# The first stage of a decoder step: DVE and ScalarE in a written order, and the dt scaling ahead of a convolution

## The chip, the cores and the metric

The kernel runs on one core of a Trainium2 chip. Time is device microseconds of one execution, and less is better. The engines are TensorE (PE in the profile, with PEld for its weight loads), VectorE (DVE), ScalarE (ACT), GpSimd (POOL) and SyncE (SP, which issues most DMAs).

## The reference

One layer of a hybrid decoder for a prompt of 1024 tokens and a sample group of 8 x 8 tokens, 1088 tokens in all, with a model width of 1024. All inputs are float32.

```python
def rmsnorm(x, g):
    y = xf * lax.rsqrt(jnp.mean(xf * xf, axis=-1, keepdims=True) + EPS)
    return y * g

h = rmsnorm(x, g1)
proj = h @ w_in                       # 1024 -> 2824 columns
u, v, bgate, cgate, hb, z, xbc, dt_raw = split(proj)
ya = chunk_mlp(gelu(u), gelu(v))      # mixer A
yb = bgate * conv3(cgate * hb)        # mixer B
xbc = silu(conv4(xbc))                # mixer C: x, B, C
dt = softplus(dt_raw + dt_bias)
y = ssd(xs, dt, -exp(a_log), Bm, Cm, state) + d_skip * xs
yc = rmsnorm(y * silu(z), ssm_norm)
x = x + concat([ya, yb, yc]) @ w_out
x = x + square(relu(rmsnorm(x, g2) @ w_ff1)) @ w_ff2
out = rmsnorm(x, final_norm)          # and the new states
```

The change is in the first stage: `rmsnorm(x, g1)`, the first columns of `h @ w_in`, and `dt_raw`.

## The kernel before

**Layout.** Activations lie transposed, features on the 128 partitions and the 1088 tokens along the free dimension. x comes as eight tiles `xt` of 128 x 1088, one for each block of 128 features (k = 0 to 7). Tokens are worked on in three chunks `CH` of 364, 364 and 360.

**Precision.** A product of float32 numbers is made of three faster ones. Each operand is split into a high part (rounded to the format of the fast product) and a low part, the rest; PE adds up high x high, low weight x high x, and high weight x low x. For x the high part is `g1 * x` rounded, written to half 0 of the tile `big`, and the low part is `g1 * x` minus it, in half 1 (L262, DVE). The high part is made by DVE for k = 0 to 2 and by ACT for k = 3 to 7 (L259 and L257). For weights `split_w` copies the high part on ACT (L100) and subtracts on DVE (L101). The first weight block, w0, is split in two pieces of 256 and 768 columns, the later ones (w1, w2, ...) in one.

**RMSNorm.** The scaling by 1/rms of a token is put off: the projection runs on `g1 * x`, and its result is multiplied by `rstd` afterwards. For `rstd`, ACT squares each x tile (L232; in place, except for k = 0, whose square starts the sum `ss`), and DVE adds the other seven squares to `ss` (L236). PE then sums `ss` over the partitions with a matrix of ones (`rms_scale`, L172), ACT takes the logarithm and the exponential (L173, L177), and DVE does one Newton step for each chunk (L180 to L183).

**The first projections.** `dt_products(k)` computes `dt_raw` from xt[k] in float32 (L247, 12 records in the profile for each k) into one bank, `psd`. The first projection (weights w0, feature block 4 of mixer C's convolution input) goes over k with all three chunks' banks open (L336 for the high weights, L340 for the low ones), so that it can follow x as it comes. `rstd` isn't known yet, so ACT copies the three banks out unscaled into a buffer `cb` (L345), and `dt_raw` into `dtT` (L347, L348). The second projection (w1, block 5) goes chunk by chunk through the helper `mm3` (L131, L132, L133); its first chunk has a bank of the pool `aps`, the others one of the three of the pool `gps`. After that chunk `rms_scale` is issued. When `rstd` is there, DVE empties the second projection's banks with the scaling in it (L293), multiplies the first projection's copies by it (L354, four products), runs the convolution of block 4 on ACT and DVE (L307, then three steps L310), multiplies `dtT` by `rstd` (L358 and L360, eight small products), and then convolves block 5. During the third projection (block 6) PE turns `dtT` to tokens on partitions (`dt_tokens`, L382 and L387), from which `softplus` makes dt.

**What sets the order.** Each engine works off its own queue in order. The order of the queues comes from a planner when the program is built: at each step an engine takes, among the instructions that the planner holds to be ready, the one that stands first in the program's text. Waits between engines are then put in. Inside `with tc.manual_schedule(engines=...)` the named engines keep the order of the text instead; before, the kernel has this only in its last stage. The x tiles, the constants `cp` and the first weights are loaded by DMAs that are all issued in the first few microseconds, and w1 and w2 behind them.

The names of the lines: L94 load of a weight block, L100 and L101 its split, L131 to L133 projection by chunks, L172 to L183 `rstd`, L232 square, L236 sum of squares, L247 dt products, L257, L259 and L262 high and low parts of x, L336 and L340 first projection, L345 its copy, L293 scaled emptying of a bank, L307 and L310 convolution, L354 scaling of the copy, L358 and L360 scaling of `dtT`, L382 dt to tokens.

Of the kernel before, what the change touches and what calls it, by code (L numbers as in the profile page):

```python
# [7 lines left out]
F32 = mybir.dt.float32  # L8
F32R = mybir.dt.float32r
BF16 = mybir.dt.bfloat16  # L10
AF = mybir.ActivationFunctionType
ALU = mybir.AluOpType
# [3 lines left out]
P = 128  # L16
D = 1024
KT = D // P
# [4 lines left out]
T = SEQ + TS  # L23
# [39 lines left out]
HC = (0, 256, 1024)  # L63
# [8 lines left out]
def body(nc, tc, I, O):  # L72
    ctx = ExitStack()
    V, S, G, PE, SY = nc.vector, nc.scalar, nc.gpsimd, nc.tensor, nc.sync
# [3 lines left out]
    whlp = ctx.enter_context(tc.tile_pool(name="whlp", bufs=2))  # L78
# [7 lines left out]
    big = bigp.tile([P, KT * 2 * T], F32R, name="big")  # L86

    def C(name):
        o, n = PCOLS[name]
        return cp[:, o:o + n]  # L90
# [3 lines left out]
        SY.dma_start(out=st, in_=src)  # L94
        return st

    def split_w(st, cuts=(0, 1024), pool=None):
        w = (pool or whlp).tile([P, 2, 1024], F32R, name="whl")
        for a, b in zip(cuts, cuts[1:]):
            S.copy(out=w[:, 0, a:b], in_=st[:, a:b])  # L100
            V.tensor_tensor(out=w[:, 1, a:b], in0=st[:, a:b], in1=w[:, 0, a:b].bitcast(F32),  # L101
                            op=ALU.subtract)
        return w

    w_plan = [I["w_in"][f] for f in W_IN_ORDER] + [I["w_out"][f] for f in range(KT)] * 2
    w_st, w_sp = {}, {}
# [5 lines left out]

    def w_split(i):
        if i < len(w_plan) and i not in w_sp:
            w_sp[i] = split_w(w_st[i], HC if i == 0 else (0, 1024))

    def next_w():

# [83 lines left out]
    rstd = statp.tile([P, T], F32, name="rstd")  # L202
# [8 lines left out]
    xg = []  # L211
    xts = []
    for k in range(KT):
        xt = midp.tile([P, 1112], F32, name="xt", tag="mid")
        xts.append(xt)
        if k == 0:
            SY.dma_start(out=xt[:, :364], in_=I["xT"][k][:, :364])
            S.dma_start(out=cp[:, :PC_A], in_=I["cpack"][:, :PC_A])
            st0 = w_st[0] = wstp.tile([P, 1024], F32, name="wst")
# [10 lines left out]
    def square(k):  # L230
        xt = xts[k][:, :T]
        S.activation(out=ss if k == 0 else xt, in_=xt, func=AF.Square)  # L232

    def add_square(k):
        if k > 0:
            V.tensor_tensor(out=ss, in0=ss, in1=xts[k][:, :T], op=ALU.add)  # L236

    V.tensor_tensor(out=wdt[:, :, 0:8], in0=C("wdt").rearrange("p (k m) -> p k m", m=8),
                    in1=C("g1").unsqueeze(2).broadcast_to([P, KT, 8]), op=ALU.mult)
# [3 lines left out]
    def dt_products(k):  # L243

        parts = [(j, 0, DTQ, j * DTQ) for j in range(4)] + [(j, DTQ, 32, SEQ + 32 * j) for j in range(2)]
        for j, o, n, t in parts:
            PE.matmul(psd[32 * j:32 * j + 32, o:o + n], wdt[:, k], xts[k][:, t:t + n],  # L247
                      start=k == 0 and o == 0, stop=k == KT - 1, skip_group_check=True)

    for k in range(KT):  # L250
        xt = xts[k]
        dt_products(k)
        b = big[:, k * 2 * T:(k + 1) * 2 * T].rearrange("p (h t) -> p h t", h=2)
        g = C("g1")[:, k:k + 1]
        for a, e in (((0, 364), (364, T)) if k == 0 else ((0, T),)):
            if k > 2:
                S.activation(out=b[:, 0, a:e], in_=xt[:, a:e], func=AF.Identity, scale=g)  # L257
            else:
                V.tensor_scalar(out=b[:, 0, a:e], in0=xt[:, a:e], scalar1=g, scalar2=None, op0=ALU.mult)  # L259
        if k == 0:  # L260
            w_split(0)
        V.scalar_tensor_tensor(out=b[:, 1], in0=xt[:, :T], scalar=g, in1=b[:, 0].bitcast(F32),  # L262
                               op0=ALU.mult, op1=ALU.subtract)
        if k:
            square(k - 1)
        if k > 2:
            add_square(k - 2)
        xg.append(b)
    w_split(1)
    square(KT - 1)  # L270
    add_square(KT - 2)
    add_square(KT - 1)

    def evac_mul(c, ps, dst, rhs=None):
        rhs = rstd if rhs is None else rhs
# [3 lines left out]
    def pad_parts(buf, pad, src, c):  # L279

        c0, n = CH[c]
        if c < 2:
            return [(buf[:, pad + c0:pad + c0 + n], src[:, :n], lambda a: a[:, c0:c0 + n])]
        m, w = SEQ - c0, NJ + pad
        sb = buf[:, pad + SEQ:pad + SEQ + NB * w].rearrange("p (b w) -> p b w", w=w)
        rows = lambda a: a.rearrange("p (b w) -> p b w", w=NJ)
        return [(buf[:, pad + c0:pad + SEQ], src[:, :m], lambda a: a[:, c0:SEQ]),
                (sb[:, :, pad:], rows(src[:, m:n]), lambda a: rows(a[:, SEQ:T]))]
# [11 lines left out]
    def conv_c(i, buf):  # L300

        sb = buf[:, 3 + SEQ:].rearrange("p (b w) -> p b w", w=11)
        G.tensor_copy(out=stC[:, i, 0:3], in_=buf[:, SEQ:SEQ + 3])
        G.tensor_copy(out=stC[:, i, 3:27].rearrange("p (b w) -> p b w", w=3), in_=sb[:, :, 8:11])
        o = midp.tile([P, 1112], F32, name="xc", tag="mid")
        w = C("sconvw")[:, i * 4:i * 4 + 4]
        S.activation(out=o, in_=buf[:, 0:1112], func=AF.Identity, scale=w[:, 0:1],  # L307
                     bias=C("sconvb")[:, i:i + 1])
        for k in range(1, 4):
            V.scalar_tensor_tensor(out=o, in0=buf[:, k:k + 1112], scalar=w[:, k:k + 1], in1=o,  # L310
                                   op0=ALU.mult, op1=ALU.add)
        S.activation(out=o, in_=o, func=AF.Silu)
        G.tensor_copy(out=xcS[:, i].rearrange("p (b w) -> p b w", w=NJ),
                      in_=o[:, 1024:1112].rearrange("p (b w) -> p b w", w=11)[:, :, 3:11])
        mids[i] = o

    def new_buf(pad, prev):
        w = NJ + pad
        buf = cbp.tile([P, 1115], F32, name="cb", tag="cb")
        G.memset(buf[:, 0:pad], 0.0)  # L320
        G.tensor_copy(out=buf[:, pad + SEQ:pad + SEQ + NB * w].rearrange("p (b w) -> p b w", w=w)[:, :, 0:pad],
                      in_=prev.rearrange("p (b w) -> p b w", w=pad))
        return buf
# [7 lines left out]
    ps0 = [gp.tile([P, 512], F32, name="gps", tag="g") for _ in CH]  # L331
# [10 lines left out]
    buf = new_buf(3, C("sst")[:, 4 * 24:5 * 24])  # L342
    for c in range(3):
        for o, i, tok in pad_parts(buf, 3, ps0[c], c):
# [4 lines left out]
    buf5 = new_buf(3, C("sst")[:, 5 * 24:6 * 24])  # L349
    gemm(next_w(), xg, range(KT), lambda c, ps: evac_pad(c, ps, buf5, 3),  # L350
         first=ap.tile([P, 512], F32, name="aps", tag="a"), hooks=[lambda: rms_scale(aslots(), catp, "yb", ss, rstd, D, False)])
    for c in range(3):
        for o, i, tok in pad_parts(buf, 3, ps0[c], c):
            V.tensor_tensor(out=o, in0=o, in1=tok(rstd), op=ALU.mult)  # L354
    conv_c(4, buf)
    for j in range(4):
        r = slice(32 * j, 32 * j + 32)
        V.tensor_tensor(out=dtT[r, :DTQ], in0=dtT[r, :DTQ], in1=rstd[r, j * DTQ:(j + 1) * DTQ], op=ALU.mult)  # L358
        if j < 2:
            V.tensor_tensor(out=dtT[r, DTQ:], in0=dtT[r, DTQ:], in1=rstd[r, SEQ + 32 * j:SEQ + 32 * j + 32],  # L360
                            op=ALU.mult)
    conv_c(5, buf5)


# [359 lines left out]
    def norm_c():  # L724
        rms_scale(aslots(), tmpp, "t", ss, rstc, 512)
        for i in range(4):
# [9 lines left out]
                    in1=C("tri").unsqueeze(1).broadcast_to([P, 4, L]), op=ALU.mult)  # L736
    wms = am.tile([TS, 4, TS], F32, name="wms")
    V.tensor_tensor(out=wms, in0=cw[:TS, 4 * L:].rearrange("p (h t) -> p h t", t=TS),
                    in1=C("btri")[:TS].unsqueeze(1).broadcast_to([TS, 4, TS]), op=ALU.mult)
# [231 lines left out]
    raw, whl = {}, {}  # L971
# [650 lines left out]
```

## Time and profile before

| | |
|---|---|
| median of 3 runs | 1129.83 us (1129.47 to 1129.85) |
| the profiled execution | 1129.33 us, of which the span is 1127.5 |
| granted clock of TensorE | 0.999 |
| PE busy | 1116.2 us, 99% of the span |
| DVE busy | 836.0 us, 74% |
| ACT busy | 497.8 us, 44% |
| first projection on PE (from 7.73 us, with dt products) | ends at about 25 us |
| second projection's first chunk | to 30.4 us |
| `rstd` complete | 40.4 us |

A row of the time-ordered view has the start and the length of a group in us, the engine, the line of the kernel, the operation, the tile written and the tiles read, shapes, the count, and, in brackets, the idle time before it with what ended it. Matmuls are pipelined and their ends are modelled, so their spacing from start to start says more than their length. In a row of the view by stretches, a busy time is followed by the number of records. In the view of one tile or line, the DMA figures are the shortest, median and longest time from issue to landing.

### The profile page before, as it was taken

The numbers are of one execution on the slowest core, as the hardware profiler recorded it, in microseconds if no ns is written. First come the engines' busy times: TensorE is split into PE (matmuls) and PEld (weight loads), VectorE is DVE, ScalarE is ACT, GpSimd is POOL, SyncE is SP. The second block draws the span as 40 slices with busy tenths as digits, with TensorE's granted clock in tenths as the row PEclk, the third lists the DMA queues.
The fourth block names the chain that finished last, engine by engine and source line by source line (L and its number), as shares of the span: only waits on it lengthen the run. The fifth ranks groups of instructions, "written<-read, shape, count | busy, mean of one in ns | idle before, by whom it ended". The sixth has DMA issues, their size and how long they took to land.

```text
span 1127.5 us, 19980 instructions
## 1 busy us (share of the span) xinstructions
PE 1116.2 (99%) x8540; PEld 1097.5 (97%) x8540; DVE 836.0 (74%) x1111; ACT 497.8 (44%) x659; POOL 57.2 (5%) x94
## 2 busy tenths in 40 slices
PE   8999999999999999999999999999999999999997
PEld 6999999999999999999999999999999999999997
DVE  8875587865656476989697497497497496599786
ACT  7536273423563344753342542442443443443544
POOL 1110020110000000000000000000000000000015
PEclk9999999999999999999999999999999999999999
DMA  6112232321037353692853953953953953953504
GB/s 258 53 57 62 64 112 102 114 79 53 23 106 266 92 216 124 287 390 79 309 200 111 401 193 122 392 192 135 389 185 137 384 188 140 391 179 138 225 1 159
DMA packets 34776, 200.43 MB, mean 178 GB/s; under 512 B 4736, under 2 KB 7680, under 8 KB 27776
## 3 DMA queue, kind: packets, MB, share of 16 engines
q1 hardware_dynamic: 32592, 196.30, 47.2%
q10 hardware_dynamic: 2096, 2.85, 0.7%
q8 instruction: 67, 1.10, 0.4%
q14 instruction: 21, 0.17, 0.0%
HBM read 175.58 MB, written 22.77 MB: 176 GB/s over the span
## 4 chain that ended last, share of the span: by engine, by line
PE 94%; DVE 3%; issue 1%; ACT 1%; DMA 1%; POOL 0%; SPq 0%; POOLq 0%; ACTq 0%; DVEq 0%
PE ps L1049 19%; PE ps L1050 19%; PE ps L1051 19%; PE gps L131 10%; PE gps L132 10%; PE gps L133 10%; PE aps L577 1%; PE aps L581 1%; DVE big L262 1%; DMA xt<-xT 1%; DVE xq L914 0%; PE p L1049 0%; PE aps L512 0%; PE ps L875 0%; PE p L1051 0%
## 5 line engine op out<-in xcount | busy, mean ns | idle before, releaser
L1049 PE MATMUL ps<-big,whl 128*128 128x272 f32 x1312 | 377.7, 288 | 0.2 <-DVE f L1131 0.2
L1050 PE MATMUL ps<-big,whl 128*128 128x272 f32 x1312 | 377.6, 288 | 0.0
L1051 PE MATMUL ps<-big,whl 128*128 128x272 f32 x1312 | 376.9, 287 | 0.0
L1049 PEld LDWEIGHTS ps<-big,whl 128*128 128x128 f32 x1312 | 247.2, 188 | 0.6 <-DVE f L1131 0.5
L1050 PEld LDWEIGHTS ps<-big,whl 128*128 128x128 f32 x1312 | 247.1, 188 | 0.0
L1051 PEld LDWEIGHTS ps<-big,whl 128*128 128x128 f32 x1312 | 246.8, 188 | 0.0
L131 PE MATMUL gps<-big,whl 128*128 128x360 f32 (+2 forms) x752 | 239.8, 319 | 0.5 <-ACT cb L345 0.5
L132 PE MATMUL gps<-big,whl 128*128 128x360 f32 (+2 forms) x752 | 236.8, 315 | 0.3 <-DVE whl L101 0.3
L133 PE MATMUL gps<-big,whl 128*128 128x360 f32 (+2 forms) x752 | 236.0, 314 | 0.0
L100 ACT CAST whl<-wq 128x1024 fp32r<-128x1024 f32 x92 | 96.5, 1050 | 221.6 <-PE ps L1051 133.8
L101 DVE TENSOR_TENSOR whl<-wq,whl 128x1024 fp32r<-128x1024 f32 x92 | 112.4, 1222 | 52.6 <-ACT whl L100 52.5
L131 PEld LDWEIGHTS gps<-big,whl 128*128 128x128 f32 x752 | 141.4, 188 | 1.8 <-ACT cb L345 1.0
L132 PEld LDWEIGHTS gps<-big,whl 128*128 128x128 f32 x752 | 141.4, 188 | 0.9 <-DVE whl L101 0.5
L133 PEld LDWEIGHTS gps<-big,whl 128*128 128x128 f32 x752 | 141.3, 188 | 0.1
L949 DVE TENSOR_TENSOR x<-x,ps 128x544 f32<-128x544 f32 x188 | 131.0, 716 | 7.7 <-PE ps L1051 6.7
L1051 PE MATMUL ps<-fo,whl 128*128 128x272 f32 x416 | 119.5, 287 | 0.0
L1049 PE MATMUL ps<-fo,whl 128*128 128x272 f32 x416 | 119.3, 287 | 0.0
L1050 PE MATMUL ps<-fo,whl 128*128 128x272 f32 x416 | 119.2, 287 | 0.0
L100 ACT CAST whl<-wst 128x1024 fp32r<-128x1024 f32 (+2 forms) x39 | 40.1, 1027 | 130.7 <-PE gps L133 81.9
L1049 PEld LDWEIGHTS ps<-fo,whl 128*128 128x128 f32 x416 | 78.3, 188 | 0.2 <-issue 0.2
L1051 PEld LDWEIGHTS ps<-fo,whl 128*128 128x128 f32 x416 | 78.2, 188 | 0.0
L1050 PEld LDWEIGHTS ps<-fo,whl 128*128 128x128 f32 x416 | 78.2, 188 | 0.0
(327 smaller groups left out, 1395.3 us busy)
## 6 DMA issues: line engine op xcount, KB each, us to landing
big<-xcd SPq DMA_DIRECT2D x47, 2176.0 KB, 9.7
wq<-w SPq DMA_DIRECT2D x66, 512.0 KB, 4.4
xcd<-big SPq DMA_DIRECT2D x7, 2176.0 KB, 7.5
wst<-w_in SPq DMA_DIRECT2D x21, 512.0 KB, 3.6
wst<-w_out SPq DMA_DIRECT2D x16, 512.0 KB, 3.6
x<-xT SPq DMA_DIRECT2D x8, 544.0 KB, 5.6
dec<-scr SPq DMA_DIRECT2D x8, 512.0 KB, 4.1
xt<-xT SPq DMA_DIRECT2D x7, 544.0 KB, 8.6
```

Source lines behind the costliest of these rows:

```text
L100: S.copy(out=w[:, 0, a:b], in_=st[:, a:b])
L101: V.tensor_tensor(out=w[:, 1, a:b], in0=st[:, a:b], in1=w[:, 0, a:b].bitcast(F32), op=ALU.subtract)
L131: PE.matmul(ps[:, :n], hi, xh, start=start, stop=False)
L132: PE.matmul(ps[:, :n], lo, xh, start=False, stop=False)
L133: PE.matmul(ps[:, :n], hi, xl, start=False, stop=stop)
L262: V.scalar_tensor_tensor(out=b[:, 1], in0=xt[:, :T], scalar=g, in1=b[:, 0].bitcast(F32), op0=ALU.mult, op1=ALU.subtract)
L577: PE.matmul(yps[hh * HD:(hh + 1) * HD, i * L:(i + 1) * L], w[:, h * HD:(h + 1) * HD], m[:, h], start=i == 0 and n == 0, stop=n == len(term ...
L581: PE.matmul(sps[:, g * 256:(g + 1) * 256], bt[:, g * P:(g + 1) * P], xw[:, g * 256:(g + 1) * 256], start=True, stop=True)
L949: V.tensor_tensor(out=out, in0=a, in1=b, op=o)
L1049: PE.matmul(o, hi, xh, start=start and k == 0, stop=False, skip_group_check=True)
L1050: PE.matmul(o, lo, xh, start=False, stop=False, skip_group_check=True)
L1051: PE.matmul(o, hi, xl, start=False, stop=k == ks - 1, skip_group_check=True)
```

## The change

The loop over k that made dt products, high part, low part, square and sum together is taken apart. `high`, `low`, `square` and `add_square` become steps of their own, and DVE and ACT are held to the order of the text in this block: dt products first in the text (they run on PE, whose order the planner still makes); high and low part of k = 0; w0's first 256 columns; the square of k = 0; high and low part of k = 1; w0's other columns; high part of k = 2, the square of k = 1, low part of k = 2; high and low parts of k = 3 to 7; the split of w1; the squares of k = 2 to 7; all sums. Which engine does which step is as before, and each step has the same size. Further down, the products of `dtT` with `rstd` come ahead of those of the first projection's copy and of the convolution of block 4, rather than behind them.

```diff
-    def split_w(st, cuts=(0, 1024), pool=None):
-        w = (pool or whlp).tile([P, 2, 1024], F32R, name="whl")
+    def split_w(st, cuts=(0, 1024), pool=None, w=None):
+        if w is None:
+            w = (pool or whlp).tile([P, 2, 1024], F32R, name="whl")
...
-            w_sp[i] = split_w(w_st[i], HC if i == 0 else (0, 1024))
+            w_sp[i] = split_w(w_st[i])
...
     for k in range(KT):
-        xt = xts[k]
-        dt_products(k)
-        b = big[:, k * 2 * T:(k + 1) * 2 * T].rearrange("p (h t) -> p h t", h=2)
+        xg.append(big[:, k * 2 * T:(k + 1) * 2 * T].rearrange("p (h t) -> p h t", h=2))
+
+    def high(k):
         g = C("g1")[:, k:k + 1]
         for a, e in (((0, 364), (364, T)) if k == 0 else ((0, T),)):
+            o, i = xg[k][:, 0, a:e], xts[k][:, a:e]
             if k > 2:
-                S.activation(out=b[:, 0, a:e], in_=xt[:, a:e], func=AF.Identity, scale=g)
+                S.activation(out=o, in_=i, func=AF.Identity, scale=g)
             else:
-                V.tensor_scalar(out=b[:, 0, a:e], in0=xt[:, a:e], scalar1=g, scalar2=None, op0=ALU.mult)
-        if k == 0:
-            w_split(0)
-        V.scalar_tensor_tensor(out=b[:, 1], in0=xt[:, :T], scalar=g, in1=b[:, 0].bitcast(F32),
-                               op0=ALU.mult, op1=ALU.subtract)
-        if k:
-            square(k - 1)
-        if k > 2:
-            add_square(k - 2)
-        xg.append(b)
-    w_split(1)
-    square(KT - 1)
-    add_square(KT - 2)
-    add_square(KT - 1)
+                V.tensor_scalar(out=o, in0=i, scalar1=g, scalar2=None, op0=ALU.mult)
+
+    def low(k):
+        V.scalar_tensor_tensor(out=xg[k][:, 1], in0=xts[k][:, :T], scalar=C("g1")[:, k:k + 1],
+                               in1=xg[k][:, 0].bitcast(F32), op0=ALU.mult, op1=ALU.subtract)
+
+    ET = mybir.EngineType
+    with tc.manual_schedule(engines={ET.DVE, ET.Activation}):
+        for k in range(KT):
+            dt_products(k)
+        high(0)
+        low(0)
+        w_sp[0] = whlp.tile([P, 2, 1024], F32R, name="whl")
+        split_w(st0, HC[:2], w=w_sp[0])
+        square(0)
+        high(1)
+        low(1)
+        split_w(st0, HC[1:], w=w_sp[0])
+        high(2)
+        square(1)
+        low(2)
+        for k in range(3, KT):
+            high(k)
+            low(k)
+        w_split(1)
+        for k in range(2, KT):
+            square(k)
+        for k in range(KT):
+            add_square(k)
...
-    for c in range(3):
-        for o, i, tok in pad_parts(buf, 3, ps0[c], c):
-            V.tensor_tensor(out=o, in0=o, in1=tok(rstd), op=ALU.mult)
-    conv_c(4, buf)
     for j in range(4):
         r = slice(32 * j, 32 * j + 32)
         V.tensor_tensor(out=dtT[r, :DTQ], in0=dtT[r, :DTQ], in1=rstd[r, j * DTQ:(j + 1) * DTQ], op=ALU.mult)
...
+    for c in range(3):
+        for o, i, tok in pad_parts(buf, 3, ps0[c], c):
+            V.tensor_tensor(out=o, in0=o, in1=tok(rstd), op=ALU.mult)
+    conv_c(4, buf)
     conv_c(5, buf5)
```

## The prediction

> **What bounds the kernel now.** I read the page's engine shares, then the chain that ended last, then TensorE's (PE's) waits over the whole span, then the first 55 us queue by queue. The first row gives, for each engine, busy time, share of the span and instructions; the second is the chain's share by engine; the rest is who PE waited for (us in total, times, longest).
>
> ```profile
> PE 1116.2 (99%) x8540; PEld 1097.5 (97%) x8540; DVE 836.0 (74%) x1111; ACT 497.8 (44%) x659; POOL 57.2 (5%) x94
> ```
> ```profile
> PE 94%; DVE 3%; issue 1%; ACT 1%; DMA 1%; POOL 0%; SPq 0%; POOLq 0%; ACTq 0%; DVEq 0%
> ```
> ```profile
> PE gps L131 <- ACT cb L345: 0.5, 1, 0.5
> PE gps L132 <- DVE whl L101: 0.3, 1, 0.3
> PE aps L382 <- DVE dtT L358: 0.3, 1, 0.3
> PE ps L875 <- POOL ss L1463: 0.3, 1, 0.3
> ```
>
> PE is the bound. A change on DVE and ScalarE (ACT) is worth what it takes from PE's waits. Later stages hold few of them (L875 is the longest of those), so what PE has gained by 60 us should reach the end. The waits that this change can touch are L131, L132 and L382. Here is PE around the first two (start, duration, line, count):
>
> ```profile
> 18.98 0.66 PE L336 MATMUL gps<-big,whl 128*128 128x364 f32 x3
> 19.57 0.69 PE L247 MATMUL aps<-xt,wdt 128*32 128x256 f32 x12
> 20.18 0.77 PE L336 MATMUL gps<-big,whl 128*128 128x364 f32 x3
> ...
> 22.78 1.16 PE L336 MATMUL gps<-big,whl 128*128 128x364 f32 x6
> 23.78 0.66 PE L340 MATMUL gps<-big,whl 128*128 128x364 f32 x3
> 24.28 0.66 PE L336 MATMUL gps<-big,whl 128*128 128x364 f32 x3
> 24.78 0.33 PE L131 MATMUL aps<-big,whl 128*128 128x364 f32 x1
> 25.64 0.80 PE L131 MATMUL gps<-big,whl 128*128 128x364 f32 x2 [0.53 <-ACT cb L345]
> 26.43 0.44 PE L132 MATMUL aps<-big,whl 128*128 128x364 f32 x1
> ```
>
> From start to start, twelve matmuls take 24.78 - 22.78 = 2.00 us, so one streams in 0.167 us, whatever its modelled duration. I count by that pitch.
>
> **Part 1: low parts sooner (high, low and squares in a written order).** Was PE short of work in the first projection? The stretch, its length, then busy time and records of PE, PEld, DVE, ACT and POOL, granted clock, DMA share and GB/s:
>
> ```profile
> 7.73:24.95 17.22, 17.22 (x154) 14.12 (x154) 17.08 (x15) 14.95 (x15) 2.27 (x2) 1.00 0.76 303
> ```
>
> No: busy 17.22 of 17.22 us, at the full granted clock. Of the 154 records 84 are dt products (seven groups of 12, each 20.18 - 19.57 = 0.61 us: 4.3) and 70 are projection matmuls (70 x 0.167 = 11.7), 16.0 in all. The missing 1.2 us go to the fifteen or so changes between dt products and projection: the three matmuls at 18.98 took 0.59 us where 0.50 is streaming. These changes follow the arrival of the input tiles, which the edit leaves alone. So low parts that come sooner feed a full engine: 0 us. If the planner put the dt products into one group, it could gain up to 1.2; if it scattered them more, it could lose as much. I take 0.
>
> **Part 2: second weights before most squares and sums.** The first projection's last matmul has streamed at 24.95 (24.78 + 0.167). Then the low part of the second weights, w1, is awaited until 26.43: 1.48 us, in which two matmuls of the next chunks (0.33) found a place. Lost: 1.15. In the written order w1 waits only for its tile and for the last high part. ACT's rows, then the landing of the x tiles, then that of the weights:
>
> ```profile
> 18.38 2.29 ACT L257 ACTIVATE big<-xt,cp 128x1088 fp32r<-128x1088 f32 x2
> 20.57 2.20 ACT L232 ACTIVATE xt<-xt 128x1088 f32<-128x1088 f32 x2
> 22.68 1.03 ACT L100 CAST whl<-wst 128x1024 fp32r<-128x1024 f32 x1
> ```
> ```profile
> 25.15 1.23 ACT L345 COPY cb<-gps 128x364 f32<-128x364 f32 x4
> ```
> ```profile
> L223 SPq DMA_DIRECT2D xt<-xT x7: 432/494/981, 1.7 to 6.0; - x7
> DMA to landing us min/median/max: 3.9/8.3/10.8
> ```
> ```profile
> 7.71 0.33 SPq L94 DMA_DIRECT2D wst<-w_in  x1
> ```
> ```profile
> DMA to landing us min/median/max: 3.5/3.9/10.3
> ```
>
> The last x tile is issued at 6.0 and none needs over 10.8 us, so it is there by 16.8; w1 is issued at 7.71 and, with 10.3 the longest of its kind, there by 18.0. ACT: last high part 16.8 to 18.0 (two in 2.29, one in 1.2), w1's high part to 19.05. DVE's rows of before:
>
> ```profile
> 22.70 1.34 DVE L262 SCALAR_TENSOR_TENSOR big<-xt,cp,big 128x1088 fp32r<-128x1088 f32 x1
> 23.96 1.28 DVE L236 TENSOR_TENSOR ss<-ss,xt 128x1088 f32<-128x1088 f32 x1
> 25.16 1.21 DVE L101 TENSOR_TENSOR whl<-wst,whl 128x1024 fp32r<-128x1024 f32 x1
> 26.30 2.67 DVE L236 TENSOR_TENSOR ss<-ss,xt 128x1088 f32<-128x1088 f32 x2
> ```
>
> So the last low part runs from 18.0 to 19.35 and w1's low part ends about 20.5, where before it ended at 26.37. PE's wait until 26.43 is gone: **-1.15 us**.
>
> **What is late next: the sums.** Before, ss ends at 28.97 and PE comes to it here:
>
> ```profile
> 30.36 1.99 PE L172 MATMUL aps<-ss,cp 128*128 128x364 f32 x6
> ```
>
> That margin of 1.39 us hid the sums. Now all seven stand behind w1's low part, each reading what the last one wrote. Followed by an independent instruction, a sum takes 1.20 (23.96 to 25.16). Two in a row take 2.67, so the second starts 1.39 after the first. Seven from 20.5 end at 20.5 + 6 x 1.39 + 1.28 = 30.1; at 1.20 each they would end at 28.95. I take 30.1, since the pair at 26.30 is the same instruction in the same dependence.
>
> [...]
>
> The squares don't hold the sums: six of them behind w1's high part, at 1.10 each, end at 19.05 + 6.6 = 25.65. ACT's copies out of the first banks (L345) start there rather than at 25.15 and are done by 26.9. PE wants those banks only after its first chunk of the second projection, which has a bank of its own and, with 24 matmuls, ends at 24.95 + 4.0 = 28.95. Later copies: 0 us, with 2 us of cover.
>
> So PE comes to L172 at 28.95, and ss is 1.15 us away. If the planner lets L172 stand right behind the chunk, PE waits all of that and part 2 is spent; if it puts matmuls of the next chunk ahead, PE waits for nothing. The trace of before can't tell; I take half: **+0.55**. Either way L172 starts at 30.1 rather than 30.36, and the chain to rstd moves by only 0.26 us.
>
> **Part 3: dt times rstd sooner.** PE, then DVE:
>
> ```profile
> 43.60 0.33 PE L133 MATMUL gps<-big,whl 128*128 128x364 f32 x1
> 44.22 0.84 PE L382 MATMUL aps<-cp,dtT 128*128 128x8 f32 x6 [0.29 <-DVE dtT L358]
> ```
> ```profile
> 39.88 0.53 DVE L183 SCALAR_TENSOR_TENSOR rstd<-rt,rstd 128x360 f32<-128x360 f32 x1
> ...
> 42.24 0.41 DVE L358 TENSOR_TENSOR dtT<-dtT,rstd 32x256 f32<-32x256 f32 x1
> ...
> 43.32 0.85 DVE L358 TENSOR_TENSOR dtT<-dtT,rstd 32x256 f32<-32x256 f32 x2
> ```
>
> PE streams until 43.77 (43.60 + 0.167) and L382 starts at 44.22: 0.45 lost to dtT. Its products run from 42.24 to 44.17 (1.93), behind those of L354. Right behind rstd they end at 40.41 - 0.26 + 1.93 = 42.1, and PE, 0.6 sooner, arrives at 43.2 (1.15 sooner at 42.6): **-0.45**. L354 and the convolution of block 4 move back by 1.93; DVE does the same work in another order, so 0 us, as long as block 5's convolution, whose input doesn't pass L354, covers block 4's first ACT step:
>
> ```profile
> 42.42 2.53 ACT L307 ACTIVATE xc<-cb,cp 128x1112 f32<-128x1112 f32 x2 [1.39 <-DVE cb L354]
> ```
>
> Without that cover DVE stands idle for one of these, 1.3 us.
>
> **The cap behind it.** A bank that DVE empties (first row, two banks) is what PE takes at 54.17:
>
> ```profile
> 53.07 0.97 DVE L293 TENSOR_TENSOR cb<-gps,rstd 128x364 f32<-128x364 f32 x2
> ```
> ```profile
> 54.17 0.43 PE L131 MATMUL gps<-big,whl 128*128 128x364 f32 x1
> ```
>
> The first bank is free at about 53.6, a margin of 0.57. DVE starts this stretch from rstd, 0.26 sooner, and has no idle time in it: PE can't be more than 0.57 + 0.26 = 0.83 us ahead at 54.17.
>
> The other queues: SP's next weight load waits for w1's low part and goes out some 6 us sooner, with nothing behind it that PE awaits so early; POOL's copies into cb wait for constants as before. 0 us.
>
> **Sum.** -1.15 + 0.55 - 0.45 = -1.05 us at 44 us, cut to -0.8 by the bank. The profiled run took 1129.33 (span 1127.5 and 1.8 around it), so 1128.5; the median of the runs is 0.5 higher, so **1129.0 us**. A measurement of this kernel can tell about 0.2%, 2.26 us, from no change; this is 0.07%.
>
> **Rivals.**
> 1. *The whole gain.* The sums end near 28.95, or PE is filled and the bank comes in time too: -1.15 - 0.45 = -1.6, 1128.2. For it: 1.20 per sum when something independent follows. Against: here nothing does.
> 2. *The change doesn't do what it says.* L172 stays right behind the chunk and PE waits until 30.1: the gain at 26.43 is given back at 30. -1.15 + 1.15 - 0.45, less where DVE is late: 0 to -0.45, 1129.4 to 1129.8.
> 3. *Slower: the late sums become the bound.* Place: L172. Rival 1's 1.6 us are gone when ss ends at 28.95 + 1.6 = 30.55, and each further us costs a us. That needs 0.45 us on my sum: one late x tile does it, with w1 and the squares queued behind its high part on ACT. A tile 1 us late gives 1130.4; DVE's 1.3 us of idleness before block 4's convolution give, by the cap, 0.83 - 1.3, so 1130.3; both about 1131. For it: ACT's fixed order. Against: the landing bounds above leave little.
> 4. *The planner re-orders PE.* It plans PE around the new order. Grouped dt products give their 1.2 us on top of rival 1: -2.8, 1127.0. Scattered ones cost 1.2 on top of rival 3: 1131.6 to 1132.2, and what moves past 60 us I can't price. For it: the dt products now come first in the text. Against: they came ahead of the projection's matmuls before, too, and wait for the same tiles.
>
> **How the numbers follow.** Forecast (-0.5 to -1.2) 0.46; whole gain 0.15; nothing 0.12; slower by the sums 0.10; planner for the better 0.09, for the worse 0.08. Faster by over 0.2% needs -2.26, which only the grouped order reaches: 0.09. Slower by over 0.2%: 0.08. Within: 0.83. The range takes in the forecast, rivals 1 and 2 and a single cause of rival 3: 1127.0 to 1130.8.
>
> **What will show it.** L101 of w1 should run near 19 to 21 us, and PE's waits for L345 and L101 vanish (part 2). PE from 7.73 to the end of the first projection should still be full, about 17.2 us (part 1). The last L236 should end near 30 at a pitch of 1.39, and L172 start there, with or without a PE wait on ss. PE's wait for dtT should vanish; a new one on L293 near 53.5 would be the cap. I am wrong if the first projection itself gets shorter by over 0.5 us, if L172 comes after 30.6, or if PE's order past 60 us differs.

## The result, and the profile after

The changed kernel takes 1136.45 us (median of 4 runs, 1135.90 to 1136.54), the kernel before 1129.82 on the same chip: a ratio of 1.0059 [1.0046, 1.0073]. It is slower by 6.6 us, outside the range that was predicted. The span of the profiled run is 1133.8 us, where it was 1127.5. In the changed kernel's file the lines of the first stage stand one lower (L101 and L102 split a weight, L132 to L134 are the projections by chunks, L173 the ones products, L237 a sum), the others as named below. Two executions further down, one of the last version (3149.01 us) and one of the kernel before beside it (1827.01 us), lie far from all the rest; the ratio is taken without them, and the two medians move by 0.04 us or less if they are left out.

TensorE's waits over the whole span that bear on the change (us in total, times, longest; the two at the kernel's start are left out):

```profile
PE gps L132 <- DVE cb L311: 4.5, 2, 4.0
PE aps L400 <- DVE dtT L372: 0.6, 1, 0.6
```

The wait for the first projection's copies (L345 before) is gone, and so is the 1.15 us of idleness at 24.95; two new waits for an emptied bank (L311, before L293) have come, of 0.5 and of 4.0 us; and the wait for `dtT`, which was to vanish, has grown from 0.29 to 0.56 us. PE's queue, row by row (start, duration, line, tile):

```profile
24.07 0.66 PE L354 MATMUL gps<-big,whl 128*128 128x364 f32 x3
...
33.22 0.32 PE L133 MATMUL gps<-big,whl 128*128 128x360 f32 x1
33.66 2.10 PE L173 MATMUL aps<-ss,cp 128*128 128x364 f32 x6
...
43.42 0.43 PE L132 MATMUL gps<-big,whl 128*128 128x364 f32 x1 [0.51 <-DVE cb L311]
...
46.24 0.83 PE L400 MATMUL aps<-cp,dtT 128*128 128x8 f32 x6 [0.56 <-DVE dtT L372]
...
58.36 0.64 PE L132 MATMUL gps<-big,whl 128*128 128x364 f32 x1 [4.02 <-DVE cb L311]
58.80 0.51 PE L133 MATMUL gps<-big,whl 128*128 128x364 f32 x1
...
62.74 0.47 PE L134 MATMUL gps<-big,whl 128*128 128x364 f32 x1
63.05 0.33 PE L132 MATMUL gps<-big,whl 128*128 128x364 f32 x1
```

The matmul that stood at 54.17 now stands at 58.36: 4.19 us later. The ones products start at 33.66, 3.30 us later than before; PE could have started them at 33.22 + 0.167 = 33.39, so they cost it 0.27 us, in which it waits for `ss`. What the first stage gained is spent before the long gap: PE begins the third projection 1.01 us sooner (38.76, before 39.77), and after the waits at 43.42 and 46.24 its second group of dt products starts at 49.00, before at 48.98. And after the gap the matmuls are slow: the fifteen from 58.36 to 63.05 take 4.69 us, where 15 x 0.167 = 2.50 would do, another 2.19. Together 6.38 us, beside 6.3 us of longer span: the whole loss stands in this stretch. The granted clock shows the second part. Windows of 2 us: length, busy time and records of PE, PEld, DVE, ACT and POOL, then the clock, DMA share and GB/s:

```profile
56.00:58.00 2.00, 0.00 (x0) 0.00 (x0) 2.00 (x3) 1.54 (x3) 1.31 (x4) 0.55 0.00 0
58.00:60.00 2.00, 1.64 (x5) 1.67 (x6) 2.00 (x7) 1.70 (x3) 1.01 (x3) 0.50 0.03 8
60.00:62.00 2.00, 2.00 (x8) 2.00 (x8) 1.69 (x2) 1.98 (x2) 0.86 (x3) 0.50 0.32 33
62.00:64.00 2.00, 2.00 (x11) 2.00 (x10) 1.67 (x3) 1.62 (x3) 0.00 (x0) 0.74 0.58 229
```

Why does the bank come so late? ACT's queue, then DVE's, from the first stage on:

```profile
20.43 0.37 ACT L365 COPY dtT<-aps 128x256 f32<-128x256 f32 x1 [2.66 <-PE aps L248]
20.70 0.18 ACT L366 COPY dtT<-aps 64x32 f32<-64x32 f32 x1
20.78 1.05 ACT L101 CAST whl<-wst 128x1024 fp32r<-128x1024 f32 x1
```
```profile
21.86 1.23 DVE L102 TENSOR_TENSOR whl<-wst,whl 128x1024 fp32r<-128x1024 f32 x1 [2.70 <-ACT whl L101]
23.00 8.27 DVE L237 TENSOR_TENSOR ss<-ss,xt 128x1088 f32<-128x1088 f32 x6
31.19 1.22 DVE L102 TENSOR_TENSOR whl<-wst,whl 128x1024 fp32r<-128x1024 f32 x1
32.32 1.28 DVE L237 TENSOR_TENSOR ss<-ss,xt 128x1088 f32<-128x1088 f32 x1
...
43.29 0.52 DVE L184 SCALAR_TENSOR_TENSOR rstd<-rt,rstd 128x360 f32<-128x360 f32 x1
...
47.63 1.22 DVE L102 TENSOR_TENSOR whl<-wst,whl 128x1024 fp32r<-128x1024 f32 x1
48.76 1.28 DVE L481 TENSOR_TENSOR ss<-rstd 128x1088 f32<-128x1088 f32 x1
49.97 7.80 DVE L328 SCALAR_TENSOR_TENSOR xc<-cb,cp,xc 128x1112 f32<-128x1112 f32 x6
57.69 0.97 DVE L311 TENSOR_TENSOR cb<-gps,rstd 128x364 f32<-128x364 f32 x2
```

The reader is to see three things. The planner put the two copies of dt into `dtT` (L365, L366), which the text has outside the written block, ahead of w1's high part on ACT; they wait 2.66 us for the last dt products on PE, and w1, its low part and all sums wait behind them. Then w2's low part, outside the block too, was put ahead of the last sum. So `ss` is complete at 32.32 + 1.28 = 33.60. And behind `rstd` DVE now makes the square of `rstd` (L481, for a later stage) before the convolutions. Before, it did so after the emptying:

```profile
53.07 0.97 DVE L293 TENSOR_TENSOR cb<-gps,rstd 128x364 f32<-128x364 f32 x2
...
55.01 1.27 DVE L463 TENSOR_TENSOR ss<-rstd 128x1088 f32<-128x1088 f32 x1
```

The first bank is free half way through the emptying's pair: 58.18 where it was 53.56, 4.62 later. Of these, 3.40 are `rstd` (43.81 against 40.41) and 1.21 are its square (48.76 to 49.97).

### The profile page after: what moved, and what is told of

Same layout as the page of the kernel before. It is cut to its first block, busy times and chain, and to the rows that moved or that the text cites. A ratio compares the mean times of both kernels' runs of the same rounds, so it can differ in the third digit from the quotient of the medians.

```text
span 1133.8 us, 19979 instructions
## 1 busy us (share of the span) xinstructions
PE 1118.1 (99%) x8540; PEld 1099.4 (97%) x8540; DVE 837.7 (74%) x1111; ACT 497.7 (44%) x659; POOL 52.3 (5%) x94
## 4 chain that ended last, share of the span: by engine, by line
PE 94%; DVE 3%; issue 1%; ACT 1%; DMA 1%; POOL 0%; SPq 0%; POOLq 0%; DVEq 0%; ACTq 0%
PE ps L1068 19%; PE ps L1067 19%; PE ps L1069 19%; PE gps L132 10%; PE gps L133 9%; PE gps L134 9%; PE aps L595 1%; PE aps L599 1%; DVE ss L237 1%; DVE xc L328 1%; DVE whl L102 1%; DMA xt<-xT 1%; PE gps L354 0%; DVE xq L932 0%; PE aps L248 0%
## 5 line engine op out<-in xcount | busy, mean ns | idle before, releaser
L132 PE MATMUL gps<-big,whl 128*128 128x360 f32 (+2 forms) x752 | 240.8, 320 | 4.5 <-DVE cb L311 4.5
L134 PE MATMUL gps<-big,whl 128*128 128x360 f32 (+2 forms) x752 | 237.3, 316 | 0.0
L101 ACT CAST whl<-wq 128x1024 fp32r<-128x1024 f32 x92 | 96.6, 1051 | 221.6 <-PE ps L1069 133.8
L102 DVE TENSOR_TENSOR whl<-wq,whl 128x1024 fp32r<-128x1024 f32 x92 | 112.3, 1221 | 51.7 <-ACT whl L101 51.5
L132 PEld LDWEIGHTS gps<-big,whl 128*128 128x128 f32 x752 | 142.3, 189 | 5.8 <-ACT xc L330 4.1
L134 PEld LDWEIGHTS gps<-big,whl 128*128 128x128 f32 x752 | 142.1, 189 | 0.1
L101 ACT CAST whl<-wst 128x1024 fp32r<-128x1024 f32 (+2 forms) x39 | 40.1, 1028 | 130.4 <-PE gps L134 81.7
```

The source lines that it names most:

```text
L132: PE.matmul(ps[:, :n], hi, xh, start=start, stop=False)
L134: PE.matmul(ps[:, :n], hi, xl, start=False, stop=stop)
```

## The experiments

The theory: the loss is the late `rstd` (through the late sums) plus the square in front of the convolutions, and both act through the wait for the bank; the gap there costs the clock on top (0.50 to 0.74 in the windows above). The rivals are named with the runs. "Before" is 1129.58 us in the first four runs, 1129.48 in the next four, 1129.32 in the three after them and 1129.33 in the last.

**The two parts alone.** The written order, with the dtT products at their old place:

```diff
+    for c in range(3): ...   # scaling of block 4's copies
+    conv_c(4, buf)
     for j in range(4): ...   # dtT products
-    for c in range(3): ...
-    conv_c(4, buf)
```

> The written order of the first stage alone; dt times rstd stays where it was before the change. Theory (DVE late): rstd is again complete near 43.8 us, 3.4 later than before, because the sums still end near 33.6. dt times rstd then ends near 47.6 and TensorE waits about 2 us for it at L400; the bank of the third projection is free near 57.0, before TensorE comes for it, so the long gap after 54 us is gone, the granted clock stays at 1.00, and the run costs the shift of rstd alone: 3.4 us, about 1133.2. Rival (the written order is harmless and the moved dt products cost it all): 1129 to 1130. Rival (the written order costs it all): 1136.4.

Measured: 1134.71 us, ratio 1.0047 [1.0032, 1.0062]. `rstd` was late as the theory said (complete at 44.21), but the gap did not go: the planner put the first dt products behind 21 matmuls of the third projection's second chunk (12 in the changed kernel), where PE waited 0.45 us for them rather than 2, so that it came to the bank before this was free at 57.4. The gap was 2.91 us, and the mean granted clock in the 12 us from 54 on was 0.86.

```profile
57.55 0.41 PE L132 MATMUL gps<-big,whl 128*128 128x364 f32 x1 [2.91 <-DVE cb L311]
```

The old first stage, with the dtT products moved:

```diff
-    for c in range(3): ...
-    conv_c(4, buf)
     for j in range(4): ...   # dtT products
+    for c in range(3): ...
+    conv_c(4, buf)
     conv_c(5, buf5)
```

> The first stage as before the change; only the products of dt with rstd ahead of the scaling and convolution of block 4. Theory: the planner puts the square of rstd (1.28 us on DVE) ahead of the convolutions, as in the changed kernel, so the bank of the third projection is emptied 1.2 us later than before, at about 54.8 rather than 53.6; TensorE, 0.45 us sooner at 44 us, waits some 1 us for it, with no loss of clock: about 0.7 us slower than before, 1130.5. What I predicted for this part alone: 0.45 us faster, 1129.4. Rival (this move costs it all): 1136.

Measured: 1130.47 us, ratio 1.0012 [1.0002, 1.0022]. The wait at the dt products is gone, and the bank costs more than that. DVE's queue and PE's row:

```profile
44.40 1.22 DVE L101 TENSOR_TENSOR whl<-wst,whl 128x1024 fp32r<-128x1024 f32 x1
45.54 1.28 DVE L463 TENSOR_TENSOR ss<-rstd 128x1088 f32<-128x1088 f32 x1
46.74 7.81 DVE L310 SCALAR_TENSOR_TENSOR xc<-cb,cp,xc 128x1112 f32<-128x1112 f32 x6
```
```profile
55.14 0.41 PE L131 MATMUL gps<-big,whl 128*128 128x364 f32 x1 [1.30 <-DVE cb L293]
```

With the products first, the scaling of block 4's copies is done only at 44.5, the convolutions wait for ACT's first step on them, and the planner filled that time with w3's low part and with the square. The second is what makes the bank late. So this part by itself loses 0.9 us. Seven of its ten executions lie at 1130.2 to 1130.7 us, three at 1131.8 to 1132.2; a piece of slow clock in the three would fit (3.4 us at 0.50, as in the last section, cost up to 1.7 us by estimate), but only one of the seven has a trace.

**Is the slow clock a matter of the gap?** The changed kernel with twenty more matmuls on PE, whose result nothing uses, between the dt products and the bank:

```diff
     def softplus():
         dt_tokens((6, 7, 8))
+        fill = ap.tile([P, 512], F32, name="aps", tag="a")
+        for u in range(20):
+            PE.matmul(fill[:, :360], w6[0][:, 0, :P], xg[0][:, 0, 728:1088], start=True, stop=True, ...)
```

> The changed kernel with 20 more matmuls on TensorE, of 0.164 us each, 3.3 us in all, into a bank that nobody reads, behind the last dt transposition of the third projection, where TensorE stands still for 4.0 us. Theory (the slow clock follows from the gap): the gap shrinks to about 0.7 us, the granted clock stays at 1.00, the 15 matmuls that took 0.304 us each take 0.167, and the run is 2 us faster with more work in it: 1134.4. Rival (the slow clock comes from elsewhere): unchanged at 1136.4, with the slow matmuls still there.

Measured: 1134.31 us, ratio 1.0045 [1.0030, 1.0060]; 0.56 us of the gap are left, and the granted clock stays at 1.00:

```profile
54.00:66.00 12.00, 11.44 (x74) 11.13 (x73) 8.74 (x13) 7.55 (x9) 2.21 (x8) 1.00 0.14 44
```

Each against its own runs of before, the loss falls from 6.63 to 4.73 us: more work on PE made the kernel 1.9 us faster, beside the 2.19 of the slow matmuls. So the clock's part is a consequence of the gap. The 20 matmuls end only when the bank is almost free, so the remaining 4.7 us is in the main the late bank.

**The chain before `rstd`.** The changed kernel with the two dtT copies at the end of the written block:

```diff
         for k in range(KT):
             add_square(k)
+        dtT = tmpp.tile(...)
+        S.copy(out=dtT[:, :DTQ], in_=psd[:, :DTQ])
+        S.copy(out=dtT[:64, DTQ:], in_=psd[:64, DTQ:DTQ + 32])
...
-    dtT = tmpp.tile(...)
-    S.copy(out=dtT[:, :DTQ], in_=psd[:, :DTQ])
-    S.copy(out=dtT[:64, DTQ:], in_=psd[:64, DTQ:DTQ + 32])
```

> The changed kernel with ScalarE's two copies of the dt products to SBUF put at the end of the written block, so that they can't stand ahead of the second weights' high part and hold it until the dt products are done. Theory: the high part runs at 18.0 to 18.5 rather than 20.8, its low part ends near 20.5 rather than 23.1, and the sums end near 31.2 (they still have the third weights' low part among them): 2.4 us sooner. The gap at the bank shrinks from 4.0 to about 3 us and TensorE goes on 2.5 us sooner: 1134.0 if the clock still drops, 1131.9 if it doesn't. Rival (these copies hold up nothing that counts): 1136.4.

Measured: 1135.05 us, ratio 1.0050 [1.0035, 1.0065], less gain than the theory had. The profiled execution is the longest of the four (1136.70 us; the shortest took 1134.32), with a gap of 3.70 us. DVE's last sum, then ACT behind the ones products:

```profile
30.44 1.28 DVE L237 TENSOR_TENSOR ss<-ss,xt 128x1088 f32<-128x1088 f32 x1
```
```profile
34.73 1.78 ACT L174 ACTIVATE rt<-aps,cp 128x364 f32<-128x364 f32 x3 [4.90 <-PE aps L173]
```

`ss` is complete at 31.72, 1.9 us sooner than in the changed kernel, and yet the ones products start at 33.92. PE was not waiting for `ss`: it was working off 51 matmuls of the second projection that the planner had put ahead of them (53 in the changed kernel, 26 in the kernel before). The theory had to be amended. What sets `rstd` here is where the planner places the ones products in PE's queue; it places them by its own reckoning of when the sums end, and PE keeps that place even when they end sooner. In the changed kernel both come close together: PE is there at 33.39, `ss` at 33.60.

The same with w2's split behind the sums as well:

```diff
             add_square(k)
+        w_load(2)
+        w_split(2)
+        dtT = tmpp.tile(...)
+        S.copy(...)   # the two copies, as above
```

> The changed kernel with the two dtT copies and the second weight of the plan (its load, high and low part) written at the end of the ordered block, behind the last sum. In the run with only the copies there, ss was complete at 31.7 but the low part of that weight still stood ahead of the last sum and the ones products behind 51 matmuls; here the sums end about 1.2 us sooner, near 30.4, and the products stand behind 39. Amended theory (the place of the ones products in TensorE's queue sets rstd): products from about 31.1, rstd complete 10.1 us later near 41.2 (43.96 with the copies alone, 43.81 in the changed kernel), the first bank emptied 2.6 us sooner than the 58.2 of the changed kernel, the gap in TensorE's row near 1.5 us and the clock kept: 1131.5 us. Rival (the wait for the bank is set by what VectorE does after rstd, whatever rstd's time): gap 3.5 to 4 us again, clock lost, 1135 us.

Measured: 1131.75 us, ratio 1.0021 [1.0012, 1.0031]. The ones products start at 31.29 behind 39 matmuls, though `ss` is complete at 30.01, and `rstd` is complete at 41.3: the amended theory to 0.2 us. The gap is 2.03 us in the profiled execution, not 1.5, and even this one cost clock there (0.86 over the 12 us from 54 on):

```profile
55.89 0.64 PE L132 MATMUL gps<-big,whl 128*128 128x364 f32 x1 [2.03 <-DVE cb L316]
```

That execution took 1132.91 us, near the upper end of the ten (1131.05 to 1132.94). The shorter ones may have kept the clock, which would be the theory's 1131.5; without their traces that is not shown.

**The chain behind `rstd`.** The changed kernel with the square of `rstd` held back on DVE until the third projection is emptied:

```diff
-    V.tensor_tensor(out=ss, in0=rstd, in1=rstd, op=ALU.mult)
+    with tc.issue_after(last6):   # last emptying of block 6
+        V.tensor_tensor(out=ss, in0=rstd, in1=rstd, op=ALU.mult)
```

> The changed kernel with rstd squared held back on VectorE until the last emptying of the third projection. Theory: this 1.28 us instruction stands between rstd and the emptying that frees the first bank, so the gap falls from 4.0 to about 2.8 us. Where a gap of that length still costs the granted clock (2.9 us did, with only the written order): 1135.2 us; where the clock holds: about 1133.2 us. Rival (something else, such as ScalarE's first convolution step, holds the emptying): gap unchanged, 1136.4 us.

Measured: 1135.11 us, ratio 1.0051 [1.0037, 1.0064]. The gap fell to 3.23 us (from 4.02) and the clock was lost for 3.4 us instead of 6.7 (0.86 over the 12 us, against 0.72 in the changed kernel). The convolutions started 0.74 us sooner, less than 1.2, since ACT's first step on block 4 then came last:

```profile
49.23 7.81 DVE L330 SCALAR_TENSOR_TENSOR xc<-cb,cp,xc 128x1112 f32<-128x1112 f32 x6 [0.32 <-ACT xc L327]
```

The same hold on the kernel that has only the dtT products moved (the two edits as above):

> The first stage of the kernel before, the dtT products moved ahead, and rstd squared held back behind the third projection's last emptying. The move alone measured 1130.47 with a gap of 1.30 us at the bank, since the planner put the third weight's low part (1.2 us) and rstd squared (1.3 us) ahead of the convolutions. Theory: without the 1.3 us in front the gap falls to nothing and the 0.29 us at the tokens stays gone: 1129.1 to 1129.4 us, at or just below the kernel before. Rival (the move itself costs through block 4's later convolution): 1130.5 us again.

Measured: 1129.55 us, ratio 1.0000 [0.9992, 1.0009], with 0.50 us at the bank. So some 0.8 of the dt part's 0.9 us is the square's place; what stays at the bank and what was gained at the dt products cancel, and the move is worth nothing.

Both ends of the chain mended at once, in the changed kernel (the dtT copies and w2's split behind the sums, and the square held back, as above):

> The changed kernel with the dtT copies and the second weight behind the sums, and rstd squared held back as well. With the first two alone TensorE stood 2.03 us at the bank and the granted clock still fell for some 3 us, 1131.75 us. Theory: without rstd squared's 1.28 us the gap is about 0.75 us and the clock holds, so 1.28 us and some 1.5 us of slow clock go: 1129.0 us (1128.6 to 1129.6). Rival (every gap at this place costs the clock): 1130.5 us.

Measured: 1130.61 us, ratio 1.0010 [1.0001, 1.0019], 1.6 us above the expectation. The gap is 1.31 us instead of 0.75, and PE waits 1.00 us at the dt products, which I had left out. The rival's number (1130.5) was met, but not by its cause, since the clock holds at 1.00 over the 12 us from 54 on:

```profile
54.76 0.40 PE L132 MATMUL gps<-big,whl 128*128 128x364 f32 x1 [1.31 <-DVE cb L318]
```

**Does the bank limit the kernel before?** The kernel before, with block 5's convolution on DVE queued behind the emptying of the third projection's first bank:

```diff
         gemm(next_w(), xg, range(KT), lambda c, ps: evac_pad(c, ps, buf, 3), hooks)
+        if i == 6:
+            with tc.issue_after(evs[-4].ins):   # emptying of the first bank
+                conv_c(5, buf5)
         conv_c(i, buf)
...
-    conv_c(5, buf5)
```

> The kernel before with one edit: the VectorE steps of block 5's convolution are queued behind the emptying of the third projection's first bank. The kernel before has a gap of 0.57 us in TensorE's row at 54.17, put down to that emptying at 53.07. If that emptying is what limits this stretch, the bank is free by about 51 and the gap goes: 1129.6 - 0.57 = 1129.0 us. Rival (the time is handed back later, since block 5's convolution comes 1 to 3 us later): 1129.6 us or more.

Measured: 1129.56 us, ratio 0.9999 [0.9990, 1.0008]. My expectation read the trace wrongly. The 0.57 us at 54.17 are a margin, from the emptying to PE's arrival; PE's row there shows no idle time. With the edit the bank is free at 51.0, and PE takes it at 54.10 as before (54.17): where PE doesn't wait, an earlier bank is worth nothing. It can pay only when PE comes sooner.

**A version from all this.** A first attempt put two of the sums between the low parts; what else it has stands in its expectation:

```diff
         for k in range(3, KT):
             high(k)
             low(k)
+            if k in (3, 5):
+                square(k)
+            if k in (4, 6):
+                add_square(k // 2 - 1)
```

> A new version, from what the runs point to: the written order kept, but with two of the seven sums between the low parts, so that the sums no longer wait for one another at the end; w1's split ahead of the other sums; the dtT copies and the second weight behind them; the dtT products first after rstd; the dt products on TensorE all behind the second chunk of the third projection; block 5's convolution behind the emptying of that projection's first bank; rstd squared behind its last. Theory: the 1.15 us that TensorE lost to w1 and the copies at the start of the second projection, and the 0.29 us at the dt products, are gained and nothing is given back at the bank: 1129.5 - 1.15 - 0.29 = 1128.1 us. Rival (the start of the kernel's later stages is set elsewhere, so that gains here are handed back): 1129.5 us.

> The same version with the dtT products at their old place, behind the scaling of block 4's copies. Theory: with the dt products on TensorE behind the second chunk, the order of these on VectorE is worth nothing: 1128.1 us, as the other. Rival (the move of the dtT products pays by itself): 0.3 us or more slower than the other.

Measured: 1133.00 us, ratio 1.0030 [1.0018, 1.0041], and 1132.91, the same ratio. That order was bad by itself: a square overwrites its x tile and so waits for the low part of the same k on DVE, and ACT's next high part waits behind it. PE ran dry in the first projection. The waits of the first of the two runs:

```profile
PE gps L372 <- ACT big L259: 1.9, 2, 1.5
PE gps L372 <- DVE big L264: 1.2, 2, 0.7
PE aps L133 <- DVE whl L102: 0.4, 1, 0.4
```

By its last dt products (57.60, before 53.58) that execution is 4.0 us behind, and its span is 4.1 us longer (1131.6 against 1127.5): the whole loss stands in the early part, so the two runs say little on the parts downstream. The medians, 0.1 us apart, show no difference by the place of the dtT products. But the losses are not made up alike. In the second run the waits for the high and low parts are 2.7 us, and the granted clock fell for 3.4 us behind a gap of 1.53 us:

```profile
26.00:28.00 2.00, 1.96 (x7) 1.96 (x8) 2.00 (x2) 2.00 (x3) 0.00 (x0) 0.56 0.00 0
28.00:30.00 2.00, 2.00 (x9) 2.00 (x8) 2.00 (x3) 1.99 (x4) 0.00 (x0) 0.59 0.00 0
```

In the first run the same gap, 1.54 us, left it at 1.00.

The second attempt keeps the changed kernel's order of sums, the mends of both ends, the early bank, and asks for the dt products later on PE:

```diff
-    for i, hooks in ((6, [lambda: dt_tokens((0, 1, 2)), lambda: dt_tokens((3, 4, 5)), softplus]), ...
+    for i, hooks in ((6, [lambda: None, lambda: dt_tokens(range(6)), softplus]), ...
```

> The changed kernel's first stage with the dtT copies and the second weight behind the sums and rstd squared held back (1130.61 us with these alone, where TensorE stood 1.00 us at the dt products and 1.31 us at the bank), and both of these waits taken away where they arise: the dt products all stand behind the second chunk of the third projection, and block 5's convolution is queued behind the emptying of that projection's first bank. The ones products stay at their place behind 39 matmuls. Theory: the 1.15 us that the earlier w1 frees at the start of the second projection and the 0.29 us at the dt products reach the end once nothing downstream stops TensorE: 1130.61 - 1.00 - 1.31 = 1128.3 us; from the kernel before, 1129.4 - 1.15 - 0.29 = 1128.0 us; faster than it by 0.09 to 0.13%. Rival (freed time at the front is handed back somewhere later, as it was in every run so far): 1129.4 us or more.

Measured: 1127.78 us (median of 10 runs), ratio 0.9986 [0.9976, 0.9995]: 1.55 us faster than the kernel before, and 8.2 faster than the changed kernel, each against its own runs of before. PE's longest waits behind the first x tiles, PE's ones products and dt products, and the clock:

```profile
PE gps L133 <- DVE whl L102: 0.3, 1, 0.3
PE ps L902 <- POOL ss L1490: 0.3, 1, 0.3
```
```profile
31.06 1.99 PE L173 MATMUL aps<-ss,cp 128*128 128x364 f32 x6
46.35 1.40 PE L406 MATMUL aps<-cp,dtT 128*128 128x8 f32 x12
```
```profile
54.00:66.00 12.00, 12.00 (x74) 12.00 (x73) 11.76 (x21) 7.73 (x8) 8.60 (x10) 1.00 0.14 44
```

The waits for the copies, for dtT and for the bank are all gone, and PE is full from 54 to 66. The 1.55 us fit the prediction's 1.15 for w1 and 0.45 for dtT, 1.60; the interval of the ratio reaches from 0.6 to 2.7 us. PE's row of the profiled execution agrees: its matmul at 52.28 is the one that stood at 54.17, 1.89 us sooner, and 0.19 of these are there at 24.09 (before 24.28), from an x tile that landed sooner (the dt products that wait for it start at 7.55, before 7.73).

## Why the prediction was wrong

**Part 1 was right.** In the changed kernel the last three matmuls of the first projection stand at 24.07, before at 24.28: the 0.21 us of difference lies within the 0.5 that the text's bound for a wrong step named. Even these are not the edit's: the dt products of the second x tile, which wait for its DMA, start at 7.53 rather than 7.73, and from there to the last three matmuls both kernels take 16.5 us. Low parts that come sooner gain next to nothing on a full engine.

**Part 2 had the right effect by a wrong step.** PE's waits at 24.95 are gone; that they are worth 1.15 us fits the last version's sum. But "In the written order w1 waits only for its tile and for the last high part" failed. A written block keeps the order of what stands in it; the planner still puts instructions from outside between them. It put the dtT copies there, and ACT stood for 2.66 us. w1's high part ran at 20.78 (predicted 18.0) and its low part ended at 23.09 (predicted 20.5). PE, which needed it at 24.7, didn't notice. The sums did.

**The sums: the pitch was right, the end was not.** Six take 8.27 us, that is 5 x 1.39 + 1.28 = 8.23, so the pair's pitch held for the whole chain, and 1.20 each did not. Their end was 33.60, predicted 30.1: 2.5 us for w1's delay and the other 1.0 for w2's low part, which the prediction had nowhere among the sums. "L172 starts at 30.1 rather than 30.36, and the chain to rstd moves by only 0.26 us" is the step that made the sign wrong: L172 (now L173) started at 33.66, and the chain moved by 3.40.

**PE at the ones products.** The 0.55 us was a choice between a wait and a fill. It was a fill, with 0.27 us of waiting left at its end. That this is the dear choice was missed: the planner let 53 matmuls pass instead of 26. With the copies last, 51 passed and the products started as late (33.92), though `ss` had been ready for 2.2 us.

**Part 3 failed at "0 us, as long as block 5's convolution, whose input doesn't pass L354, covers block 4's first ACT step".** It did not cover. ACT stood until block 4's copies were scaled (L378) and did both blocks' first steps only then:

```profile
47.80 2.53 ACT L325 ACTIVATE xc<-cb,cp 128x1112 f32<-128x1112 f32 x2 [7.79 <-DVE cb L378]
```

The 1.3 us of idleness that the text named as the other case was filled by the planner with other work, of which the square of `rstd` lies on the way to the bank. Alone this part was +0.9 us where -0.45 stood. In the changed kernel even the -0.45 did not come: the dtT products ended at 46.18 (predicted 42.1) behind the late `rstd`, and PE waited 0.56 us for them.

**The cap was the right place with the wrong sign.** The bank was taken as a limit on the gain, 0.83 us, with DVE starting that stretch 0.26 us sooner. DVE started it 3.4 us later, and the same bank became the loss.

**The granted clock was not in the sum.** It is a third of the loss, 2.2 us, and the run with the fill gave 1.9 of them back.

Rival 3 came nearest: late sums, decided from 30.55 on. Its 1128.2 + (33.60 - 28.95) = 1132.85 lacks the square (1.21) and the clock (2.19); with them it is 1136.25, and 1136.45 was measured. That it comes so close is partly luck, for its place was wrong: PE waits 0.27 us for `ss` at the ones products, and the loss arises at the bank 25 us later. It was held unlikely on the landing times of the x tiles, and these were not the cause.

What is shown and what is argued: that the copies, w2's split and the square of `rstd` make most of the loss is shown by moving them. The loss is 6.63 us as changed, 5.47 with the copies last, 2.27 with w2's split last too, 5.63 with only the square held back, and 1.29 with all three. That the planner places the ones products by a reckoning of its own is read from the queues of these kernels, not tried by itself. That the slow clock follows from the gap is shown by filling the gap.

## What to carry to other kernels

A written order for two engines orders only what is inside it: list everything that the planner could put in between, and what that waits for, and write it behind the chain that matters. Where a chain ends in an engine with a queue of other work, read its place in that queue, not the time at which its input is ready. And when PE gets time back early on, follow the next two waits downstream before you book it: here the gain was real only once the bank and the dt products no longer stopped PE.

## What the runs showed of the hardware

The price of a gap on PE was not its length alone. Over the same 12 us window, from 54 to 66, slow time is 12 x (1 - clock) / 0.5, since the windows of 2 us show a granted clock that falls to 0.50:

| run | gap at the bank | mean clock, 54 to 66 | slow time |
|---|---|---|---|
| dt part alone | 1.30 us | 1.00 | 0 |
| both ends mended | 1.31 | 1.00 | 0 |
| copies and w2 last | 2.03 | 0.86 | 3.4 us |
| written order alone | 2.91 | 0.86 | 3.4 |
| square held back | 3.23 | 0.86 | 3.4 |
| copies last | 3.70 | 0.72 | 6.7 |
| changed kernel | 4.02 | 0.72 | 6.7 |

```profile
54.00:66.00 12.00, 7.98 (x39) 7.89 (x39) 10.61 (x16) 8.82 (x9) 3.19 (x8) 0.72 0.15 45
```

The row is the changed kernel's. The slow time is 3.4 us in three of these runs and 6.7 in two, each time in one stretch, and among these runs the step from none to 3.4 us lies between a gap of 1.31 and one of 2.03 us. But the length of a gap does not decide it: in the two runs of the first attempt, gaps of 1.54 and 1.53 us, each 0.8 us behind a smaller one of 0.70, cost nothing in one execution and a piece of 3.4 us in the other. While it lasts in the changed kernel, matmuls follow at (62.74 - 58.80) / 13 = 0.303 us instead of 0.167.

What decides whether a gap of some 1.5 us costs a piece of slow clock or nothing is not shown by these runs. The gaps are those of one profiled execution each.
